# Expert weights of the second 128 tokens through a DRAM table instead of one-hot products

## The chip, the cores and the metric

The kernel runs on one core of a Trainium2 chip. The metric is device time in microseconds (us) of one execution. The engines are called by the profile's names: PE is TensorE's matmuls, PEld its weight loads, DVE is VectorE, ACT is ScalarE, POOL is GpSimd and SP is SyncE, which issues most DMA transfers. Each engine works through its instructions in the order in which the built program lists them.

## What is computed

One decoder layer for 256 tokens of width 1024, all in float32: a modulated norm, an input projection, retention and sparse attention, an output projection, then a second norm and an expert layer, and a last norm. The change lies in the expert layer, which is this, for 128 tokens at a time:

```python
q = (hblk @ w_q).reshape(B, TB, PEER_HEADS, 2, PEER_DHALF)
s = jnp.einsum('btphd,phnd->btphn', q, subkeys)
v, i = lax.top_k(s, PEER_TOPK)
cand = (v[..., 0, :, None] + v[..., 1, None, :])          # 16 x 16 sums per head
cidx = (i[..., 0, :, None] * PEER_NKEYS + i[..., 1, None, :])
tv, tj = lax.top_k(cand, PEER_TOPK)
eidx = jnp.take_along_axis(cidx, tj, axis=-1)
w = jax.nn.softmax(tv, axis=-1)
a = jax.nn.gelu(jnp.einsum('btd,btpkd->btpk', hblk, w_down[eidx]))
return jnp.einsum('btpk,btpkd->btd', w * a, w_up[eidx])
```

Each token has 8 heads with 16 experts each, out of 16384 experts. Within a head the 16 are all different; two heads of a token can choose the same expert, and then their weights add up.

## The kernel before

No expert's rows are gathered. The kernel goes through all 16384 experts in 128 tiles of 128, and multiplies with dense weights that are zero for experts that a token did not choose. The dense weights V lie in SBUF as 128 tiles (128 experts x 256 tokens): `VL` holds tiles 0 to 63, `VH` tiles 64 to 127.

The expert layer consists of units, in the order of the list `seq`: 16 query units (`wq`), 128 `down` units, 128 `up` units. Each unit reads 512 KB of weights (`load`, SP's queue, tile `raw`, three buffers), which ACT and DVE split into a rounded part `H` and a rest `L` (`split`, four buffers each), and then runs its products on PE three times (H, L and the other operand's rest). A `down` unit makes 24 matmuls of 256 columns, the gelu of a tile, and puts it into V or multiplies it in. An `up` unit takes V's tile, splits it into `a1` and `a2`, and makes 12 matmuls of 512 columns into four accumulators `acc_o`.

Beside the units two generators run, a piece at a time, by credits (a `wq` unit gives 1.7, a `down` unit 1.1 in the first phase and 1.15 in the second):

- `top_gen` (phase "top") finds the top 16 of each half of the product keys, sorts 50 candidate sums of each head (`top16`), and gets the chosen expert's number: a one-hot `oh` over 50 candidates for 16 places (128x800), its product `oe` with the candidates' numbers on POOL (L946), and the sum `ev` of that on DVE. A head's piece costs 2.1 credits. Then the softmax, and tables of the experts' high and low halves of seven bits and of the weights, transposed by PE. First tokens 0 to 127, then 128 to 255.
- `w_gen` (phase "w") turns the tables into V: for four tokens at a time one-hots `o1`, `o0` over 128 (DVE), their product with the weights in two parts `ow` (DVE and ACT), eight matmuls of 128 columns into bank `w`, and a copy or product into V. 64 groups for 256 tokens, 1.4 credits each.

When `w_gen` is through (phase "up"), the rest of `seq` becomes up and down units in turn, and then up units alone.

The order on each engine is the framework's: in the expert layer a scheduler lists the instructions by its own estimate, may move them forward past others, and puts in the waits; `issue_after` keeps the pieces of `top_gen` behind the last `L`. DVE, ACT and PE follow program order only where `order["on"]` names them, which in the expert layer is nowhere but in the tail. Most instructions of these engines carry line 80 (81 after the change), that of a helper, so the profile is read by tiles.

Of the kernel before, what the change touches and what calls it, by code (L numbers as in the profile page):

```python
# [24 lines left out]
F32 = mybir.dt.float32  # L25
# [11 lines left out]
P = 128  # L37
T = 256
# [18 lines left out]
SPL = 1  # L57
CT = 1.1
# [5 lines left out]
def build(tc, I, out, dbg=None, stop=None):  # L64
# [5 lines left out]
    class Ordered:  # L70
        """An engine whose instructions stay in program order while order["on"] has its name."""
# [52 lines left out]
    csd = mk(dpool, (1, D), F32, "csd")  # L124

# [105 lines left out]
    # 2 silu(c) on every partition  # L231
# [36 lines left out]
    # norm 1: the product that transposes a row block scales it too  # L268
# [38 lines left out]
    # projection blocks A (q | kc ks kw vc) and B (rq | vs vw gate)  # L307
# [92 lines left out]
    def rope(dst, src, tab, tt, nh, dh, v=0):  # L400
        """dst (SBUF) = rotated src (PSUM), nh heads of dh."""
# [24 lines left out]
    def half(c, post, nf=0):  # L426
        """A projection block of 512 columns; post(i) after each of its four units."""
# [81 lines left out]
    # NSA transposes  # L509
# [22 lines left out]
    # compressed keys and values  # L532
# [74 lines left out]
    # NSA attention  # L607
# [27 lines left out]
    def attn_unit(tt, p):  # L635
        """The scaled probabilities of heads p and 4 + p, transposed."""
# [74 lines left out]
    # retention: scores transposed, decayed  # L711
# [10 lines left out]

    nsa(0)
    nsa(1)

    # retention: values, group norm, swish gate
# [43 lines left out]
    # output projection, residual, norm 2: one half of the tokens after the other  # L770
# [79 lines left out]
    # ------------------------------------------------------------------- PEER  # L850
# [3 lines left out]
    vls = mk(vlo, (P, (NT // 2 + 4) * T), F32, "VL")  # L854
# [8 lines left out]
    tab = small[:, :T].bitcast(F16).rearrange("p (a b) -> p a b", a=2)  # L863
    tabw = small[:, T:T + T // 2].bitcast(F16)
    tabl = small[:, 2 * T:3 * T]
    iow = small[:, 3 * T:4 * T].bitcast(F16).rearrange("p (a b) -> p a b", b=WG)

    subT = mk(tk, (P, 16, P), F32, "subT")
    ioi = mk(tk, (P, P, WG), I32, "ioi")
    with tc.issue_after(spill.ins):  # L870
        nc.gpsimd.dma_start(subT, I["subT"])
        G.iota(ioi, pattern=[[1, P], [0, WG]], base=0, channel_multiplier=0)
    V.tensor_copy(iow, ioi)
    ioj = mk(tk, (P, NCAND, 16), BF, "ioj")
# [37 lines left out]
    def top_gen(sc):  # L912
        """Top 16 of each product key half, then of each head's candidates; then the tables."""
# [7 lines left out]
        for tt in range(2):  # L921
# [17 lines left out]
            pend = None  # L939
            for p in range(8):  # L940
                top16(cand[:, p, :], tv[:, p, :], tp[:, p, :], NCAND, "s3")
                V.tensor_copy(tpf[:, p, :], tp[:, p, :])
                oh = mk(tk, (P, NCAND, 16), BF, "oh", bufs=2)
                V.tensor_tensor(oh, ioj, tpf[:, p:p + 1, :].to_broadcast([P, NCAND, 16]), op=ALU.is_equal)
                oe = mk(tk, (P, NCAND, 16), F32, "oe", bufs=3)
                G.tensor_tensor(oe, oh, cidx[:, p, :, None].to_broadcast([P, NCAND, 16]), op=ALU.mult)  # L946
                if pend is not None:
                    V.tensor_reduce(ev[:, p - 1, :], pend.rearrange("p j k -> p k j"), axis=AX.X, op=ALU.add)
                pend = oe
                yield 2.1  # L950
            V.tensor_reduce(ev[:, 7, :], pend.rearrange("p j k -> p k j"), axis=AX.X, op=ALU.add)
            # softmax over the 16, its maximum first in the sorted values
            ex = mk(tk, (P, 8, 16), F32, "ex", bufs=2)
# [6 lines left out]
            ei = mk(tk, (P, P), I32, "ei", bufs=2)  # L960
            V.tensor_copy(ei, ev.rearrange("p a b -> p (a b)"))
            e1 = mk(tk, (P, 2, P), I32, "e1", bufs=2)
            V.tensor_scalar(e1[:, 0, :], ei, 7, None, op0=ALU.arith_shift_right)
            V.tensor_scalar(e1[:, 1, :], ei, 127, None, op0=ALU.bitwise_and)
            ef = mk(tk, (P, 2, P), F32, "ef", bufs=2)
# [8 lines left out]
            wt = mk(tk, (P, P), F32, "wt", bufs=2)  # L974
            S.activation(wt, b[:, 2, :], AF.Copy, scale=WSC)
            dump(f"e{tt}", ev)
            dump(f"w{tt}", ex)
            # the scaled weights in two parts of float16's precision
# [3 lines left out]

    def w_gen(ohp):
        """The dense weights of every expert and token, four tokens at a time, into VL and VH."""
        half = NT // 2
        for gi in range(T // 4):
# [47 lines left out]
    def gate_unit(m):  # L1034
        """A part of the second gate, in the place of weights that are used up; its row goes to DRAM."""
# [19 lines left out]
    def up_units(js, ap):  # L1055
        """Some experts' contributions, one half of the tokens after the other."""
        ops = []
        for j in js:
            h, l = splits.pop(("up", j))
            v = vtile(j)  # L1060
            a1 = mk(ap, (P, T), F32R, "a1", bufs=3)
# [6 lines left out]
        for tt in range(2):  # L1068
            tq = slice(tt * P, (tt + 1) * P)
            for hf in range(2):  # L1070
                # the very last sums in two halves, so that the first can go on
# [8 lines left out]
    # the order of the units on the tensor engine  # L1080
# [13 lines left out]
    def load_to(i):  # L1094
        while issued_u[0] <= i and issued_u[0] < len(seq):
            u = seq[issued_u[0]]
            load(u, I[u[0]][u[1]])
            issued_u[0] += 1
# [9 lines left out]

    gen = None
# [9 lines left out]
    while i < len(seq):  # L1119
# [20 lines left out]
        while gen is not None and credit > 0:  # L1140
            try:
# [11 lines left out]
                else:  # L1153
# [6 lines left out]
                    # the units already loaded stay first; then up and down in turn  # L1160
# [14 lines left out]
    # the tail: gated residual and the last norm  # L1175
# [87 lines left out]
def host_arrays(i):  # L1263
    """The inputs as the program reads them (layouts only) and constants of the shapes."""
# [56 lines left out]
```

## Time and profile before

| | us |
|---|---|
| median of 3 runs | 1040.93 |
| lowest and highest run | 1040.06, 1041.23 |
| span of the profiled execution, first to last instruction | 1037.9 |
| PE busy | 1009.2 (97%) |
| DVE busy | 760.4 (73%) |
| ACT busy | 606.8 (58%) |
| POOL busy | 61.5 (6%) |

The page gives the profiled execution's span and not its time from outside; the runs lie 2.2 to 3.3 us above that span. PE's busy time is that of pipelined matmuls with modelled ends, so a busy PE may still wait a little inside. The DMA engines moved 199 MB, 192 GB/s on average, most of it through SP's queue.

### The profile page before, as it was taken

What the parts mean: (1) busy time and instruction counts of PE and PEld (TensorE: products, weight loads), DVE (VectorE), ACT (ScalarE), POOL (GpSimd) and SP (SyncE); (2) the same over time, 40 slices, a digit from 0 to 9 for tenths busy, and PEclk for the clock granted to TensorE, in tenths of its full rate; (3) what the DMA queues carried; (4) which work ended last, traced back from release to release, by engine and by line L of the source; (5) the groups of instructions that cost most, each with busy time, mean ns of one, the idle gap of its engine ahead of it and who ended that gap; (6) DMA issues with size and microseconds to landing.
All of it is one profiled execution on the core that took longest, in us unless ns stands there. A gap on an engine that the chain in (4) does not pass through costs nothing.

```text
span 1037.9 us, 17713 instructions
## 1 busy us (share of the span) xinstructions
PE 1009.2 (97%) x6580; PEld 902.1 (87%) x6582; DVE 760.4 (73%) x1653; ACT 606.8 (58%) x1244; POOL 61.5 (6%) x53
## 2 busy tenths in 40 slices
PE   7999999999998889999999999999999999999995
PEld 6876687999998889999999999988888888888884
DVE  7988888899778786667777777665955556565665
ACT  7544884555436357777777777645445555545453
POOL 1040000000331310000000000000000000000001
PEclk9999999999999999999999999999999999999998
DMA  9998753546555444444444444567976666666661
GB/s 367 352 350 335 244 181 136 168 152 183 168 149 174 144 152 135 151 147 143 148 142 144 143 143 143 156 230 231 317 234 193 197 190 214 190 199 188 198 189 57
DMA packets 56184, 199.19 MB, mean 192 GB/s; under 512 B 7305, under 2 KB 7585, under 8 KB 55713
## 3 DMA queue, kind: packets, MB, share of 16 engines
q1 hardware_dynamic: 55200, 193.59, 58.3%
q0 software_dynamic: 752, 4.20, 1.1%
q8 instruction: 51, 0.84, 0.3%
q14 instruction: 37, 0.30, 0.1%
q10 hardware_dynamic: 144, 0.26, 0.1%
HBM read 195.92 MB, written 2.11 MB: 191 GB/s over the span
## 4 chain that ended last, share of the span: by engine, by line
PE 84%; DVE 9%; POOL 3%; ACT 1%; issue 1%; DMA 0%; SPq 0%; DVEq 0%; POOLq 0%; ACTq 0%
PE acc L80 54%; PE dn L80 9%; PE w L80 7%; PE C L80 5%; PE O L80 4%; POOL oe L946 3%; PE S L80 3%; PE T L80 2%; DVE ev L80 2%; DVE L L80 2%; DVE oh L80 1%; DVE tp L80 1%; DVE VL L80 1%; DVE adaraw L80 0%; DMA xn<-in_x_dram 0%
## 5 line engine op out<-in xcount | busy, mean ns | idle before, releaser
L80 DVE TENSOR_TENSOR L<-raw,H 128x1024 fp32r<-128x1024 f32 x284 | 346.4, 1221 | 119.5 <-ACT H L80 114.9
L80 ACT ACTIVATE H<-raw 128x1024 fp32r<-128x1024 f32 x284 | 300.0, 1058 | 172.4 <-PE acc L80 132.6
L80 PE MATMUL acc<-H,a 128*128 128x512 f32 (+1 forms) x1030 | 315.9, 388 | 0.0
L80 PE MATMUL acc<-hH,H 128*128 128x256 f32 x800 | 230.8, 289 | 0.0
L80 PE MATMUL acc<-hH,L 128*128 128x256 f32 x800 | 226.6, 283 | 3.3 <-DVE L L80 3.3
L80 PEld LDWEIGHTS acc<-H,a 128*128 128x128 f32 x1030 | 193.0, 188 | 39.9
L80 PE MATMUL acc<-hL,H 128*128 128x256 f32 x800 | 226.6, 283 | 0.0
L80 PE MATMUL acc<-L,a 128*128 128x512 f32 (+1 forms) x515 | 199.7, 388 | 0.0
L80 PEld LDWEIGHTS acc<-hH,L 128*128 128x128 f32 x800 | 152.9, 191 | 4.1 <-DVE L L80 4.1
L80 PEld LDWEIGHTS acc<-hH,H 128*128 128x128 f32 x800 | 153.5, 192 | 0.1
L80 PEld LDWEIGHTS acc<-hL,H 128*128 128x128 f32 x800 | 153.2, 192 | 0.2 <-DVE hL L80 0.2
L80 PEld LDWEIGHTS acc<-L,a 128*128 128x128 f32 x515 | 96.7, 188 | 19.7
L80 ACT ACTIVATE ow<-o,VL 128x128 f16<-128x128 f16 x256 | 104.5, 578 | 5.2 <-DVE o L80 5.2
L80 PE MATMUL dn<-hH,L 128*128 128x256 f32 x352 | 99.8, 283 | 4.4 <-DVE L L80 4.4
L80 PE MATMUL dn<-hH,H 128*128 128x256 f32 x352 | 101.5, 288 | 0.4 <-ACT H L80 0.4
L80 PE MATMUL dn<-hL,H 128*128 128x256 f32 x352 | 99.6, 283 | 0.0
L80 PEld LDWEIGHTS dn<-hH,L 128*128 128x128 f32 x352 | 67.3, 191 | 5.0 <-DVE L L80 5.0
L80 PE MATMUL w<-ow,o 128*128 128x128 f16 x512 | 71.0, 296 | 0.0
L80 PEld LDWEIGHTS dn<-hH,H 128*128 128x128 f32 x352 | 67.6, 192 | 0.6 <-ACT H L80 0.6
L80 PEld LDWEIGHTS dn<-hL,H 128*128 128x128 f32 x352 | 67.4, 192 | 0.0
L80 PEld LDWEIGHTS <-o 128*128 128x128 f16 x512 | 51.9, 118 | 3.4
L80 DVE TENSOR_TENSOR ow<-o,VL 128x512 f16<-128x512 f16 x64 | 26.9, 420 | 36.9 <-PE w L80 36.9
(333 smaller groups left out, 1213.5 us busy)
## 6 DMA issues: line engine op xcount, KB each, us to landing
raw<-in_down_dram SPq DMA_DIRECT2D x128, 512.0 KB, 3.6
raw<-in_up_dram SPq DMA_DIRECT2D x128, 512.0 KB, 3.7
adaraw<-in_wadaT_dram SPq DMA_DIRECT2D x40, 512.0 KB, 8.0
raw<-in_wq_dram SPq DMA_DIRECT2D x16, 512.0 KB, 3.7
raw<-in_win_C_dram SPq DMA_DIRECT2D x12, 512.0 KB, 5.2
rawA<-in_win_A_dram SPq DMA_DIRECT2D x8, 512.0 KB, 9.6
raw<-in_wout_dram SPq DMA_DIRECT2D x8, 512.0 KB, 4.7
VL<-in_wadaT_dram SPq DMA_DIRECT2D x8, 512.0 KB, 4.6
```

The source lines that it names most:

```text
L80: i = fn(*a, **kw)
L946: G.tensor_tensor(oe, oh, cidx[:, p, :, None].to_broadcast([P, NCAND, 16]), op=ALU.mult)
```

## The change

Only tokens 0 to 127 keep the one-hots of `w_gen` (32 groups instead of 64). For tokens 128 to 255:

- A table `wd2` of 16384 x 128 float32 (8.4 MB) lies in DRAM, one row for each expert and one column for each of these tokens. It is filled with zeros by eight transfers of 1 MB from a tile `zero`, issued on POOL's queue.
- `top_gen` takes these tokens first. It sorts all heads (0.8 credits each), does the softmax into `exd`, and then finds a head's expert numbers (1.8 credits each), with `oe` on DVE instead of POOL. For tokens 128 to 255 the number times 128 plus the token gives the address `eid`, and `put_weights` adds the head's weights to the table: 16 indirect transfers on POOL's queue, each with 128 addresses of 4 bytes (one for each token). The 16 of a head may run together; the next head's wait until they have landed.
- With each load of an `up` tile goes a read of 128 rows of the table (64 KB, tile `wt2`, two buffers) on SP's queue, which waits for the last head's additions. `up_units` multiplies V's columns 128 to 255 by it.
- `down` units put the gelu of tokens 128 to 255 straight into V.

```diff
+    wd2 = mk(dpool, (NT * P, P), F32, "wd")
+    wd = wd2.rearrange("a (b o) -> (a b) o", o=1)
...
+    zero = mk(pe_, (P, ZC), F32, "zero")
+    G.memset(zero, 0.0)
+    wz = wd2.rearrange("(p a) b -> p (a b)", p=P)
+    for i in range(NT * P // ZC):
+        G.dma_start(wz[:, i * ZC:(i + 1) * ZC], zero)
...
-        for tt in range(2):
+        for tt in (1, 0):
...
-                oe = mk(tk, (P, NCAND, 16), F32, "oe", bufs=3)
-                G.tensor_tensor(oe, oh, cidx[:, p, :, None].to_broadcast([P, NCAND, 16]), op=ALU.mult)
-                if pend is not None:
-                    V.tensor_reduce(ev[:, p - 1, :], pend.rearrange("p j k -> p k j"), axis=AX.X, op=ALU.add)
-                pend = oe
-                yield 2.1
+                yield 0.8
...
+            for p in range(8):
+                oh = mk(tk, (P, NCAND, 16), BF, "oh", bufs=2)
+                V.tensor_tensor(oh, ioj, tpf[:, p:p + 1, :].to_broadcast([P, NCAND, 16]), op=ALU.is_equal)
+                oe = mk(tk, (P, NCAND, 16), F32, "oe", bufs=2)
+                V.tensor_tensor(oe, oh, cidx[:, p, :, None].to_broadcast([P, NCAND, 16]), op=ALU.mult)
+                V.tensor_reduce(ev[:, p, :], oe.rearrange("p j k -> p k j"), axis=AX.X, op=ALU.add)
+                if tt:
+                    V.tensor_scalar(ev[:, p, :], ev[:, p, :], float(P), tokf, op0=ALU.mult, op1=ALU.add)
+                    V.tensor_copy(eid[:, p, :], ev[:, p, :])
+                    put_weights(p)
+                yield 1.8
+            if tt:
+                continue
...
+    def put_weights(p):
+
+        group = []
+        for k in range(16):
+            i = G.indirect_dma_start(wd, bass.IndirectOffsetOnAxis(ap=eid[:, p, k:k + 1], axis=0),
+                                     exd[:, p, k:k + 1], None, compute_op=ALU.add)
+            for o in group:
+                tc.declare_no_dep(i.ins, o.ins, reason="a head's places all differ")
+            for o in placed:
+                tc.add_manual_dep(i.ins, o.ins.name, sync, reason="the head before has been added")
+            group.append(i)
+        placed[:] = group
...
-        for gi in range(T // 4):
+        for gi in range(P // 4):
...
+            V.tensor_tensor(v[:, P:], v[:, P:], wts.pop(j), op=ALU.mult)
...
+            if u[0] == "up":
+                w = mk(apool, (P, P), F32, "wt2", bufs=2)
+                i_ = Q.dma_start(w, wd2[u[1] * P:(u[1] + 1) * P, :])
+                for o in placed:
+                    tc.add_manual_dep(i_.ins, o.ins.name, sync, reason="all heads have been added")
+                wts[u[1]] = w
```

In the built program three places show what moved. The first is POOL's queue at the program's start, before the first rope (tile `kn`); `cs_p` and `keys` are tiles that the attention clears, `csd` is a copy of a row to DRAM. Before:

```order
L534 MEMSET kcT_772 128x32
L626 MEMSET cs_p_949 128x256
L196 MEMSET epsd_85 128x1
L277 DMA csd_73<-cs_98 16x1x64
L413 TENSOR_TENSOR kn_579<-sq_596 128x384
```

After:

```order
L537 MEMSET kcT_773 128x32
L727 MEMSET zero_934 128x2048
L629 MEMSET cs_p_960 128x256
L730 DMA wd_74<-zero_934 128x2048 x8
L280 DMA csd_73<-cs_99 16x1x64
L199 MEMSET epsd_86 128x1
L416 TENSOR_TENSOR kn_580<-sq_597 128x384
```

The zeros stand in the code behind the retention scores, but go out at the very start, before anything that POOL waits for.

The second place is SP's queue at the loads of `down` tiles 45 to 49 (units 61 to 65), with the semaphores that each row waits for; DMAHW are SP's own transfers, DMASW those of POOL's queue. Before:

```order
L80 DMA raw_4336<-in_down_dram 128x1024 [waits DMAHW3_49,DVE_49]
L80 DMA raw_4368<-in_down_dram 128x1024 [waits DMAHW4_49,DVE_49]
L80 DMA raw_4412<-in_down_dram 128x1024 [waits DMAHW5_49,DVE_49]
L80 DMA raw_4444<-in_down_dram 128x1024 [waits DMAHW6_49,DVE_49]
L80 DMA raw_4491<-in_down_dram 128x1024 [waits DMAHW7_49,DVE_49]
```

After:

```order
L81 DMA raw_4475<-in_down_dram 128x1024 [waits DMAHW4_49,DVE_49]
L81 DMA raw_4512<-in_down_dram 128x1024 [waits DMAHW5_49,DVE_49]
L81 DMA raw_4549<-in_down_dram 128x1024 [waits DMAHW6_49,DVE_49]
L81 DMA wt_1250_6984<-wd_74 128x128 [waits DMASW4_49,DMASW3_49,DMASW5_49,DMASW2_49,DMASW6_49,DMASW1_49,DMASW7_49,DMASW0_49,PE_49]
L81 DMA wt_1261_7056<-wd_74 128x128
L81 DMA raw_4581<-in_down_dram 128x1024 [waits DMAHW7_49,DVE_49]
L81 DMA raw_4618<-in_down_dram 128x1024 [waits DMAHW0_49,DVE_49]
```

The reads of the table were moved forward from the up units to here, some 40 units earlier: the two `wt2` buffers take the place of `exd` and `eid`. The values waited for are those after the last of the 128 additions.

The third place is DVE's queue at the same units, in the last heads of the top phase. Before:

```order
L80 TENSOR_TENSOR L_4415<-raw_4292,H_4414 128x1024 [waits DMAHW7_49,PE_49,Activation_49]
L80 CAST tpf_3899<-tp_3898 128x16 [waits DVE_49]
L80 TENSOR_TENSOR oh_4407<-ioj_1964,tpf_3899 128x800 [waits DVE_49]
L80 TENSOR_TENSOR L_4447<-raw_4336,H_4446 128x1024 [waits DMAHW0_49,PE_49,Activation_49]
L80 TENSOR_REDUCE ev_3900<-oe_4409 128x16 [waits Pool_49]
```

After:

```order
L81 TENSOR_TENSOR L_4584<-raw_4475,H_4583 128x1024 [waits DMAHW0_49,PE_49,Activation_49]
L81 TENSOR_TENSOR oh_4613<-ioj_1981,tpf_4075 128x800
L81 TENSOR_TENSOR oe_4615<-oh_4613,cidx_3994 128x800 [waits DMASW4_49,DMASW3_49,DMASW5_49,DMASW2_49,DMASW6_49,DMASW1_49,DMASW7_49,DMASW0_49,DVE_49]
L81 TENSOR_TENSOR L_4621<-raw_4512,H_4620 128x1024 [waits DMAHW1_49,PE_49,Activation_49]
L81 TENSOR_REDUCE ev_4076<-oe_4615 128x16 [waits DVE_49]
L81 TENSOR_TENSOR VL_1963<-VL_1963,wt_1250_6984 128x128 [waits DMAHW3_49]
L81 TENSOR_TENSOR VL_1963<-VL_1963,wt_1261_7056 128x128 [waits DMAHW4_49]
L81 TENSOR_TENSOR L_4653<-raw_4549,H_4652 128x1024 [waits DMAHW2_49,PE_49,Activation_49]
```

DVE no longer waits for POOL's `oe`, but for all transfers of POOL's queue, ahead of the L of unit 62; the products with the table's tiles follow there.

## Rows read from the trace of the kernel before

**Rows 1.** The page's first part: busy us, share of the span, instructions.

```profile
PE 1009.2 (97%) x6580; PEld 902.1 (87%) x6582; DVE 760.4 (73%) x1653; ACT 606.8 (58%) x1244; POOL 61.5 (6%) x53
```

**Rows 2.** Stages: length, busy us (instructions) of each engine, PEclk, DMA share, GB/s.

```profile
183.00:262.00 79.00, 79.00 (x664) 78.81 (x663) 74.10 (x310) 40.91 (x68) 1.30 (x1) 1.00 0.55 167
262.00:315.00 53.00, 50.41 (x416) 49.80 (x415) 41.72 (x101) 24.42 (x37) 17.22 (x8) 1.00 0.50 150
315.00:325.00 10.00, 9.33 (x78) 9.33 (x79) 10.00 (x37) 5.35 (x12) 0.00 (x0) 1.00 0.74 244
325.00:382.00 57.00, 50.62 (x410) 49.17 (x410) 45.38 (x108) 25.01 (x40) 19.25 (x8) 1.00 0.48 143
382.00:662.00 280.00, 280.00 (x2345) 276.56 (x2344) 201.81 (x449) 212.48 (x556) 0.00 (x0) 1.00 0.48 145
...
678.00:1024.00 346.00, 346.00 (x1530) 286.51 (x1530) 213.63 (x273) 173.51 (x256) 3.10 (x6) 1.00 0.66 207
```

**Rows 3.** Chain that ended last, top phase: start us, us, engine and tile.

```profile
291.87 1.56 DVE ev L80
...
296.31 2.42 POOL oe L946
298.75 1.54 DVE ev L80
```

**Rows 4.** The same chain in the one-hot stage.

```profile
384.88 0.95 PE w L80 x8
385.83 2.87 PE dn L80 x24
```

**Rows 5.** The same chain in the prefix, two rounds of k.

```profile
28.69 1.38 PE O L80 x6
...
33.56 1.38 PE O L80 x6
```

**Rows 6.** Stretches of the prefix, columns as in rows 2.

```profile
17.50:20.90 3.40, 3.21 (x16) 2.30 (x15) 3.23 (x5) 3.37 (x6) 0.00 (x0) 1.00 1.03 412
...
24.30:55.00 30.70, 30.70 (x151) 25.93 (x151) 28.57 (x51) 16.17 (x26) 0.00 (x0) 1.00 0.93 345
55.00:100.00 45.00, 44.80 (x238) 28.64 (x238) 38.47 (x93) 19.35 (x51) 10.99 (x9) 1.00 0.93 358
100.00:183.00 83.00, 80.66 (x516) 62.22 (x516) 69.93 (x164) 59.99 (x148) 2.12 (x3) 1.00 0.58 191
```

**Rows 7.** DVE by form, 255 to 385 us: busy, mean ns | idle before, releaser.

```profile
L80 DVE TENSOR_TENSOR L<-raw,H 128x1024 fp32r<-128x1024 f32 x40 | 48.5, 1218 | 2.8 <-ACT H L80 1.4 <-issue 1.3
L80 DVE TENSOR_REDUCE ev<-oe 128x16 f32<-128x800 f32 x16 | 24.8, 1550 | 20.4 <-POOL oe L946 20.4
...
L80 DVE CAST tpf<-tp 128x16 bf16<-128x16 uint32 x16 | 2.7, 167 | 0.1
...
L80 DVE TENSOR_TENSOR VL<-wt,VL 128x128 f32<-128x128 f32 x1 | 0.3, 283 | 0.0
```

**Rows 8.** POOL's instructions in order of time: start, us [idle before, releaser].

```profile
0.88 0.53 POOL L395 MEMSET sq<- 128x512 f32 x1
...
8.47 0.68 POOL L277 DMA_DIRECT2D csd<-cs  x1 [3.82 <-DVE t L80]
...
179.62 0.54 POOL L871 DMA_DIRECT2D subT<-in_subT_dram  x1
...
303.18 2.40 POOL L946 TENSOR_TENSOR oe<-oh,cidx 128x800 f32<-128x800 bf16 x1 [4.46 <-DVE oh L80]
310.11 1.56 POOL L946 TENSOR_TENSOR oe<-oh,cidx 128x800 f32<-128x800 bf16 x1 [4.52 <-DVE oh L80]
```

**Rows 9.** DMA issues: count, KB each, median us from issue to landing.

```profile
out_dram<-VL SPq DMA_DIRECT2D x3, 256.0 KB, 2.0
...
csd<-cs POOLq DMA_DIRECT2D x1, 4.0 KB, 5.0
```

**Rows 10.** DVE in order of time, beside POOL's oe of 310.11 us.

```profile
311.70 1.53 DVE L80 TENSOR_REDUCE ev<-oe 128x16 f32<-128x800 f32 x1 [1.73 <-POOL oe L946]
```

More of the change, by code (lines that the diff above doesn't have):

```diff
@@ L57 @@
 SPL = 1
+ZC = 2048
 CT = 1.1
@@ L853, in build @@
     vlo = es.enter_context(tc.tile_pool(name="vlo", bufs=1, reuse_waits="tile"))
-    vls = mk(vlo, (P, (NT // 2 + 4) * T), F32, "VL")
+    vls = mk(vlo, (P, NT // 2 * T + 576), F32, "VL")
     VL = vls[:, :NT // 2 * T].rearrange("p (a b) -> p a b", a=NT // 2)
@@ L862, in build @@
     WG = 4
[L863 to L866, printed above, removed]
+    tab = small[:, :P].bitcast(F16).rearrange("p (a b) -> p a b", a=2)
+    tabw = small[:, P:P + P // 2].bitcast(F16)
+    tabl = small[:, 192:320]
+    iow = small[:, 320:576].bitcast(F16).rearrange("p (a b) -> p a b", b=WG)
     subT = mk(tk, (P, 16, P), F32, "subT")
     ioi = mk(tk, (P, P, WG), I32, "ioi")
+    tok = mk(tk, (P, 1), I32, "tok")
+    tokf = mk(tk, (P, 1), F32, "tokf")
     with tc.issue_after(spill.ins):
@@ L872, in build @@
         G.iota(ioi, pattern=[[1, P], [0, WG]], base=0, channel_multiplier=0)
+        G.iota(tok, pattern=[[P, 1]], base=0, channel_multiplier=1)
     V.tensor_copy(iow, ioi)
+    V.tensor_copy(tokf, tok)
+    exd = mk(tabs, (P, 8, 16), F32, "exd")
+    eid = mk(tabs, (P, 8, 16), I32, "eid")
     ioj = mk(tk, (P, NCAND, 16), BF, "ioj")
@@ L938, in top_gen @@
             ev = mk(tk, (P, 8, 16), F32, "ev", bufs=2)
-            pend = None
             for p in range(8):
@@ L942, in top_gen @@
                 V.tensor_copy(tpf[:, p, :], tp[:, p, :])
-                oh = mk(tk, (P, NCAND, 16), BF, "oh", bufs=2)
-                V.tensor_tensor(oh, ioj, tpf[:, p:p + 1, :].to_broadcast([P, NCAND, 16]), op=ALU.is_equal)
-                oe = mk(tk, (P, NCAND, 16), F32, "oe", bufs=3)
-                G.tensor_tensor(oe, oh, cidx[:, p, :, None].to_broadcast([P, NCAND, 16]), op=ALU.mult)
-                if pend is not None:
-                    V.tensor_reduce(ev[:, p - 1, :], pend.rearrange("p j k -> p k j"), axis=AX.X, op=ALU.add)
-                pend = oe
-                yield 2.1
-            V.tensor_reduce(ev[:, 7, :], pend.rearrange("p j k -> p k j"), axis=AX.X, op=ALU.add)
-            ex = mk(tk, (P, 8, 16), F32, "ex", bufs=2)
+                yield 0.8
+            ex = exd if tt else mk(tk, (P, 8, 16), F32, "ex", bufs=1)
             V.tensor_tensor(ex, tv, tv[:, :, 0:1].to_broadcast([P, 8, 16]), op=ALU.subtract)
@@ L959, in top_gen @@
             V.tensor_tensor(ex, ex, sm[:, :, None].to_broadcast([P, 8, 16]), op=ALU.mult)
-            ei = mk(tk, (P, P), I32, "ei", bufs=2)
+            for p in range(8):
[11 more added lines that the diff above has]
+                continue
+            ei = mk(tk, (P, P), I32, "ei", bufs=1)
             V.tensor_copy(ei, ev.rearrange("p a b -> p (a b)"))
-            e1 = mk(tk, (P, 2, P), I32, "e1", bufs=2)
+            e1 = mk(tk, (P, 2, P), I32, "e1", bufs=1)
             V.tensor_scalar(e1[:, 0, :], ei, 7, None, op0=ALU.arith_shift_right)
             V.tensor_scalar(e1[:, 1, :], ei, 127, None, op0=ALU.bitwise_and)
-            ef = mk(tk, (P, 2, P), F32, "ef", bufs=2)
+            ef = mk(tk, (P, 2, P), F32, "ef", bufs=1)
             V.tensor_copy(ef, e1)
@@ L973, in top_gen @@
             S.activation(tab[:, :, tq], b[:, 0:2, :], AF.Copy)
-            wt = mk(tk, (P, P), F32, "wt", bufs=2)
+            wt = mk(tk, (P, P), F32, "wt", bufs=1)
             S.activation(wt, b[:, 2, :], AF.Copy, scale=WSC)
-            dump(f"e{tt}", ev)
-            dump(f"w{tt}", ex)
             V.tensor_copy(tabw[:, tq], wt)
@@ L981, in top_gen @@
             yield 1.0
+    sync = mybir.DependencyInfo(mybir.DependencyClass.Sync, mybir.DependencyReason.DATA)
+    placed = []
+    def put_weights(p):
[9 more added lines that the diff above has]
+        placed[:] = group
     def w_gen(ohp):
         half = NT // 2
-        for gi in range(T // 4):
+        for gi in range(P // 4):
             t0 = gi * 4
@@ L1107, in split_to @@
             splitted[0] += 1
+    wts = {}
     gen = None
```

## Prediction

> **What bounds the kernel now.** The busy shares come first [rows 1]: TensorE (PE) is busy for 97% of the span. That is an average, so the stages come next, all at full granted clock [rows 2]. Before 183 us stands the prefix. From 183 to 262 us PE has no idle time. From 262 to 382 us (the rest of the selection of experts, called top phase below) it idles for 2.6 + 0.7 + 6.4 = 9.6 us. From 382 to 662 us (one-hots) and from 678 to 1024 us (up products) it has none. The chain of waits tells who sets the pace in the top phase [rows 3]: not PE but VectorE (DVE), in a ring of L, oh, POOL's oe and ev that comes round every 298.75 - 291.87 = 6.88 us, once a head. After 382 us the chain is PE alone [rows 4]: a down unit takes 2.87 us, a group of four tokens' one-hot products 0.95 us. In the prefix PE follows a period of 33.56 - 28.69 = 4.87 us for one k [rows 5], and the DMA engines are just as full: share 1.03 from 17.5 to 20.9 us and 0.93 from 24.3 to 100 us [rows 6]. So PE's work pays one for one after 382 us, DVE's work counts from 262 to 382 us, and DMA bytes count before 100 us.
>
> **One-hots for 128 tokens only.** 32 of the 64 groups of `w_gen` go. Each has 0.95 us of PE on the chain [rows 4], and PE has no idle time there [rows 2]: 32 x 0.955 = 30.6 us are gained. DVE's and ACT's share of these groups was hidden and gives nothing.
>
> **The top phase.** `oe` moves from POOL to DVE. In the ring DVE idles for 20.4 / 16 = 1.3 us a head, waiting for POOL, and works 5.6 us, two L among it [rows 7]. The product over 800 elements lies between the row of 128 (283 ns) and L's of 1024 (1218 ns) [rows 7]; on the line between them it is 0.98 us. Half of the heads get two short operations more, each near the 167 ns of the cast [rows 7]. By the code's credits a head now spans 2.6 / 1.1 = 2.36 units instead of 1.91, so 0.36 L (0.4 us) are added: 5.6 + 0.98 + 0.4 = 7.0 us, or 7.3 with the short operations, for 2.36 units, that is 3.0 to 3.1 us for a unit. PE wants 2.87. DVE falls behind by 0.17 us in each of 16 x 2.36 = 38 units, 6.4 us, while the four L buffers let it run 4 x 2.87 = 11.5 us ahead. So PE's idle 9.6 us should go (bounds: none of it or all of it; I take all, since 6.4 is under 11.5).
>
> **Read-back and the extra product.** 128 products of 128x128 on DVE at 0.283 us [rows 7] make 36 us, 128 reads of 64 KB make 8.4 MB, and a down unit's gelu stays in two pieces on ACT. From 382 us on DVE works 201.8 of 280 us and 213.6 of 346 us, ACT less than 77%, the DMA engines 0.48 to 0.66 [rows 2]. I cost all three at nothing. If that cover is gone, it is in the one-hot stage: DVE at 72% plus about two products in 3.83 us (15%) would be near 87%; I allow 0 to 8 us.
>
> **The zeros.** The order shows POOL's memset and the eight writes of 1 MB ahead of everything that POOL waits for. A memset of 512 columns takes 0.53 us [rows 8], so the one of 2048 takes about 2 us and the writes start near 6.5 us. 8.39 MB at 350 to 410 GB/s [rows 6] is 20 to 24 us of all DMA engines, in a stretch where 0.07 of 31 us, some 2 us, are to spare up to 55 us, and where PE and DMA are equally full. DVE's second rope, an ACT copy and SP's load of `wv` wait for the end of the writes, so they can't spread over the later, emptier stretch; and from 55 to 183 us PE idles for only 2.5 us [rows 6], so a late start is not won back. I take 20 us, with 10 (writes that fit the gaps better) and 28 (rows of 8 KB that hold off loads of 4 KB rows, and so the first k) as ends.
>
> **The 128 indirect additions and who waits for them.** POOL issues 16 for a head and then waits until these have landed. It starts when the first `eid` is ready, with L of unit 32 (16 query units and then down units, counted from 0). Two queues wait for the last of the 128. SP waits at the first read of the table, behind unit 63's load: all further weight loads stand behind it. DVE waits after unit 61's L. That is 29 units after the start, far ahead of the up units for which the table is read, because the scheduler moved the reads and products up to the place where memory becomes free. 29 units at 3.04 us are 88 us, and PE lives for some 6 us more from L tiles in store: 94 us are covered. When the wait ends, DVE has an oe (0.98) and an L (1.22) ahead of PE: 3 us with ACT's part.
>
> What POOL needs is not in the trace; I bound it from both sides. Issue: at least the 0.54 us of a plain transfer of 128 rows; the row that is cut into small pieces (csd) took 0.68 us [rows 8]. At most 2.4 us, POOL's longest instruction over 128 partitions [rows 8]. Landing: 2.0 us, as for the output, to 5.0 us, as for csd's 4 KB [rows 9]. POOL is slower beside DVE: oe took 1.56 us when DVE stood still for it and 2.40 us when an L ran beside it [rows 8, 10], a factor of 1.54. DVE is nearly always busy here. I take 0.68 x 1.54 = 1.04 us, since 128 addresses of 4 bytes are nearest to csd's pieces, and 3.5 us, the middle, to land: 128 x 1.04 + 8 x 3.5 = 161 us. PE stands still for 161 - 94 = 67 us.
>
> The Trainium skill (SBUF — State Buffer, "SBUF: two separate sides") says that DVE and GpSimd share a port pair under an exclusive lock, and that descriptors written by GpSimd starve under it. The trace agrees as far as the two times of oe go; no row shows it for a transfer. Without that factor the sum would be 128 x 0.68 + 28 = 115 us and the stall 21 us.
>
> **Sum.** 1037.9 - 30.6 - 9.6 + 20 + 67 + 3 = 1087.7 us of span. The median of the runs is 3.0 us above the profiled span (1040.93), so about **1091 us**. A measurement of this kernel tells some 0.2% (2 us) from no change.
>
> **Rivals.**
> 1. *The additions are cheap, and the kernel is faster.* Issue 0.54 and landing 2.0 us give 128 x 0.54 + 16 = 85 us, less than the 94 covered. No stall, nothing to refill: 1037.9 - 40.2 + 20 + 3.0 = **1021 us**. It decides below 111 us for all 128 (0.65 us each with 3.5 us to land), where the stall and its 3 us eat the 20 us that remain. For it: POOL's direct transfers in [rows 8]. Against it: none of them has 128 separate destinations, and DVE was not saturated beside them. Chance 0.20. The Trainium skill (DMA: Bandwidth & Descriptors, "Anatomy of one DMA — SWDGE (gpsimd) path") speaks for this case: about 2.0 us fixed for a transfer, and many descriptors before their making counts. No run here shows it for indirect ones yet.
> 2. *The additions are heavy*, since each reads DRAM before it writes, or POOL reads addresses slowly: 2.4 us each and 5.0 us to land are 128 x 2.4 + 40 = 347 us, a stall of 253 us and **1277 us**. For it: POOL's slow rows beside DVE. Against it: eight transfers may be under way at once. Chance 0.18 for anything above 1200 us or near it.
> 3. *The zeros are hidden* and the stall is as forecast: 1091 - 20 = **1071 us**. For it: DMA shares under 1.0 from 24 us on. Against it: PE's period and the DMA engines' are equal there. Chance 0.12.
> 4. The forecast, with a stall of 20 to 150 us: 0.50.
>
> **How the numbers follow.** The cheap case reaches up to the border of no change, so faster by over 0.2% has 0.19, within 0.2% 0.03 (the narrow band near 111 us), slower 0.78. The range from 1019 to 1200 us takes in the cheap case at its price and POOL times up to some 270 us (1.9 us each with 3.5 us to land); what is left out is most of rival 2 and a little below 1019. The bounds of the zeros (10 to 28) and of the read-back (0 to 8) lie inside.
>
> **What would show it.** In the profile after: a hole of PE, DVE, ACT and SP together near 380 to 450 us, its end released by POOL's queue, and POOL's indirect transfers one behind the other from about 300 us; their mean time decides between 1, 2 and the forecast. The first query unit near 203 us instead of 183 and a k period above 4.87 us for the zeros. No POOL in the ring of the top phase, and PE without gaps up to the hole. 256 matmuls of `w` instead of 512 and down units every 3.83 us behind the hole. Wrong would be: a PE without the hole, a hole that begins elsewhere (a wait that I did not find), or up units slower than before, which I cost at nothing.

## The result, and the profile after

The changed kernel takes **1208.6 us** (median of 4 runs, 1206.2 to 1212.6) against 1040.5 us before: a ratio of 1.162 (95% interval 1.160 to 1.165), slower. The forecast was 1091 us with 1019 to 1200 as range: the sign and the place of the loss were right, the size was not.

The page of the changed kernel, its span, busy shares and some of the lines of 40 slices (30.1 us each), stands against [rows 1]:

```profile
span 1205.6 us, 17346 instructions
...
PE 986.8 (82%) x6323; PEld 879.0 (73%) x6323; DVE 746.2 (62%) x1647; ACT 555.1 (46%) x1077; POOL 241.3 (20%) x175
...
PE   5799999999999000000999999999999999999996
...
DVE  4788887999997000001887786655855555555556
...
POOL 3030000000877777777000000000000000000001
PEclk7899999999999555555999999999999999999998
```

PE is busy 22 us less than before and the span is 168 us longer. The slices show why: six of them are empty on PE, and DVE does nothing in five of these and a tenth in the sixth, while POOL works on. Five stretches (length, busy us and instructions of PE, PEld, DVE, ACT and POOL, then granted clock, DMA share, GB/s) answer to [rows 2, 6]:

```profile
25.00:50.00 25.00, 18.50 (x66) 14.59 (x67) 12.98 (x21) 8.73 (x14) 0.00 (x0) 0.75 1.02 420
225.00:375.00 150.00, 150.00 (x1256) 150.00 (x1255) 146.30 (x478) 78.28 (x119) 58.78 (x32) 1.00 0.66 173
388.00:571.00 183.00, 1.44 (x13) 1.24 (x11) 1.42 (x2) 0.00 (x0) 141.28 (x91) 0.51 0.21 1
571.00:600.00 29.00, 25.38 (x192) 25.06 (x193) 26.99 (x52) 15.22 (x32) 0.00 (x0) 0.90 0.76 236
600.00:625.00 25.00, 25.00 (x211) 24.72 (x211) 19.33 (x48) 21.22 (x56) 0.00 (x0) 1.00 0.57 164
```

The first is the zeros: DMA full at 420 GB/s, PE short of weights and at a granted clock of 0.75. The second is the top phase, in which PE no longer idles. The third is the hole. The fourth is its tail: 192 matmuls in 29 us, where the fifth, the same work at full pace, makes 211 in 25. Who holds the engines in the hole is told by the waits between 380 and 580 us (engine, tile, what it waited for: us, times, longest):

```profile
ACT H L81 <- DMA raw<-in_down_dram: 191.8, 3, 190.4
DVE oe L81 <- DMA wd<-exd,eid: 186.3, 1, 186.3
PEld acc L81 <- DVE L L81: 182.5, 1, 182.5
PE acc L81 <- DVE L L81: 182.3, 1, 182.3
```

PE waits for an L of DVE; DVE waits for the indirect transfers, but **in front of an oe**, an instruction of the selection that touches no table. ACT waits for weights, because SP stands at its first read of the table. POOL in order of time, around the start of the fourth head (start, us, [idle before, releaser]), answers to [rows 8]:

```profile
377.83 3.68 POOL L1007 DMA_INDIRECT wd<-exd,eid  x1 [0.30 <-issue]
381.82 2.43 POOL L1007 DMA_INDIRECT wd<-exd,eid  x1 [0.31 <-issue]
384.55 1.55 POOL L1007 DMA_INDIRECT wd<-exd,eid  x1 [0.30 <-issue]
...
406.83 1.55 POOL L1007 DMA_INDIRECT wd<-exd,eid  x1 [0.30 <-issue]
410.85 1.55 POOL L1007 DMA_INDIRECT wd<-exd,eid  x1 [2.46 <-issue]
```

From the moment DVE stands still (383.3 us) every later transfer takes 1.55 to 1.57 us and 0.30 us pass before the next. Between heads 2.4 to 2.6 us pass, in which POOL waits for the landing. Beside a busy DVE a transfer took up to 3.68 us. The first starts at 300.06 us. The chain that ended last (start, us, what) has the last one together with its landing, and behind the hole a read of the table:

```profile
566.28 3.03 DMA wd<-exd,eid
...
587.18 4.57 DMA wt<-wd
```

So the last has landed at 569.3 us: POOL needs 269 us for the 128.

### The profile page after: what moved, and what is told of

The parts are those of the page before. It is cut to its first block, busy times and chain, and to the rows that moved or that the text cites. A ratio compares the mean times of both kernels' runs of the same rounds, so it can differ in the third digit from the quotient of the medians.

```text
span 1205.6 us, 17346 instructions
## 1 busy us (share of the span) xinstructions
PE 986.8 (82%) x6323; PEld 879.0 (73%) x6323; DVE 746.2 (62%) x1647; ACT 555.1 (46%) x1077; POOL 241.3 (20%) x175
## 3 DMA queue, kind: packets, MB, share of 16 engines
q0 software_dynamic: 20336, 12.66, 7.1%
## 4 chain that ended last, share of the span: by engine, by line
PE 45%; DMA 4%; DVE 3%; issue 1%; POOL 1%; ACT 0%; DVEq 0%; SPq 0%; ACTq 0%
PE acc L81 33%; PE dn L81 10%; DMA wt<-wd 3%; PE w L81 3%; DVE L L81 1%; POOL wd L1007 1%; DVE VL L81 1%; DMA raw<-in_down_dram 0%; DVE VH L81 0%; DVE ev L81 0%; DMA wd<-exd,eid 0%; ACT VL L81 0%; DVE oe L81 0%; DVE r30v L81 0%; ACT H L81 0%
## 5 line engine op out<-in xcount | busy, mean ns | idle before, releaser
L81 PE MATMUL acc<-hH,L 128*128 128x256 f32 x616 | 175.8, 285 | 182.3 <-DVE L L81 182.3
L1007 POOL DMA_INDIRECT wd<-exd,eid x128 | 211.3, 1651 | 156.6 <-DVE exd L81 100.1
L81 PE MATMUL acc<-hH,H 128*128 128x256 f32 x616 | 178.6, 291 | 0.0
L81 PE MATMUL acc<-hL,H 128*128 128x256 f32 x616 | 175.8, 286 | 0.0
L81 PE MATMUL dn<-hH,H 128*128 128x256 f32 x536 | 152.9, 285 | 1.4 <-ACT g L81 1.4
L81 PE MATMUL dn<-hL,H 128*128 128x256 f32 x536 | 151.7, 283 | 0.0
L81 PE MATMUL dn<-hH,L 128*128 128x256 f32 x536 | 151.7, 283 | 0.0
L81 PEld LDWEIGHTS dn<-hH,H 128*128 128x128 f32 x536 | 102.9, 192 | 3.7 <-ACT g L81 2.5
L81 PEld LDWEIGHTS dn<-hL,H 128*128 128x128 f32 x536 | 102.7, 192 | 1.2
L81 DVE SCALAR_TENSOR_TENSOR adaraw<-adaraw,cs 128x1024 f32<-128x1024 f32 x40 | 48.3, 1216 | 12.4 <-DMA adaraw<-in_wadaT_dram 12.4
```

Of the source, the lines that this page charges most:

```text
L81: i = fn(*a, **kw)
L1007: i = G.indirect_dma_start(wd, bass.IndirectOffsetOnAxis(ap=eid[:, p, k:k + 1], axis=0), exd[:, p, k:k + 1], None, compute_op=ALU.add)
```

## The experiments

First the two waits. In the built program exd has bytes 88064 to 88576 and eid 89088 to 89600 of each partition, and the sixth oe of the *first* 128 tokens was packed into 88448 to 91648. That place is free only when the last addition has read its operands. The text on the order above gave the place of exd and eid to the two `wt2` buffers instead; in the built program the first of these lie at bytes 166272 and up, on tiles of H. So there are two causes to take apart: the place of the oe, and the reads of the table that were moved some 40 units forward on SP.

**a1_reads_late**: each read on SP behind its own unit's weight load.

```
-                i_ = Q.dma_start(w, wd2[u[1] * P:(u[1] + 1) * P, :])
+                with tc.issue_after(last["load"].ins):
+                    i_ = Q.dma_start(w, wd2[u[1] * P:(u[1] + 1) * P, :])
```

> The changed kernel with one edit: each read of the table stands on SP's queue behind its own up unit's weight load, so no read and no product is moved forward. Theory P (the prediction's words: both queues wait because the scheduler moved the reads and products forward): both waits go with the reads to the first up unit, near 550 us; the additions end near 570 us there, so the hole of 182 us shrinks to 20 to 50 us and the time is 1050 to 1080 us. Theory S (the wait on DVE has nothing to do with the reads: in the built program the sixth oe of the first 128 tokens has SBUF bytes 88448 to 91648 of each partition, and exd and eid, which the additions read, have 88064 to 88576 and 89088 to 89600, so the packer gave this oe a place that is free only after the last addition): the hole stays, from about 388 to 570 us, and the time is 1200 to 1215 us.

Measured: 1223.0 us (ratio 1.176, 1.173 to 1.178). The hole stays:

```profile
DVE oe L81 <- DMA wd<-exd,eid: 184.4, 1, 184.4
```

Theory S holds, the prediction's account of DVE's wait falls: the reads are not what DVE waits for. The 14 us on top of the changed kernel's time are lost later, in the up stage, where PE idles for 5.7 us between 1000 and 1200 us and makes 807 matmuls there (the changed kernel 884 from 980 to 1180 us); a4, d1 and e1 below show why.

**a2_own_place**: exd and eid as columns of VL's tile, made 256 columns wider for them, that nothing takes later; the reads stay moved forward.

```
-    exd = mk(tabs, (P, 8, 16), F32, "exd")
-    eid = mk(tabs, (P, 8, 16), I32, "eid")
+    exd = small[:, 576:704].rearrange("p (a b) -> p a b", a=8)
+    eid = small[:, 704:832].bitcast(I32).rearrange("p (a b) -> p a b", a=8)
```

> The changed kernel with one edit: exd and eid get bytes of their own at the end of VL's tile (1 KB a partition), which nothing takes later; the reads of the table stay where they were moved, 40 units ahead. Theory: DVE no longer waits, but SP still waits at the first read with all later weight loads behind it, and three raw and four H and L tiles in store let PE go on for at most 7 units more (20 us): hole from 388 to 410 us until 570 us, 1190 to 1215 us. Rival (SP's wait is covered by what is loaded, DVE's place alone made the hole): hole under 50 us, below 1080 us.

Measured: 1209.9 us (ratio 1.163, 1.161 to 1.166). The same hole with another holder:

```profile
DVE VL L81 <- DMA wt<-wd: 193.3, 15, 182.8
ACT H L81 <- DMA raw<-in_down_dram: 234.1, 27, 188.0
```

Now it is SP's read with the weights behind it, and on DVE a product with the table that was moved forward; no oe waits any more. The rival is out.

**a3_both**: both edits.

> Both edits at once: own place for exd and eid, and each read behind its own up load. Theory: each of two waits alone makes the hole, so only both together take it away; then the first queue that waits is SP at the first up unit, near 550 us. POOL's additions end near 570 us if they keep the 1.86 us of the hole (8 x 32 us from 300 us), or 580 to 600 us if they take longer beside a busy DVE: a hole of 20 to 50 us, 1040 to 1075 us. Rival (accumulating transfers slow every queue of DMA while they run, so the weights come late): hole small, but PE below full from 390 to 570 us, above 1080 us.

Measured: 1085.3 us (ratio 1.043, 1.040 to 1.047), 10 us above the expected band. One hole is left, in front of the first up unit, where PE works 9.39 of 50 us:

```profile
550.00:600.00 50.00, 9.39 (x67) 9.19 (x66) 5.21 (x10) 4.97 (x12) 29.89 (x20) 0.59 0.28 34
```

So either wait alone keeps the whole hole, and only both together remove it: 123 us went. Before that hole PE is at full (24.9 to 25.0 of each 25 us from 400 to 550 us) while POOL adds, so the additions don't hold up the weights.

**a4_both_ups_last**: a3, and all down units before the up units.

```
-                        new += [("up", j), uu]
-                        j += 1
+                        new.append(uu)
```

> Both edits, and all down units stand before all up units, so the first read of the table comes near 690 us. Theory: no hole at all; the changed kernel's 1208 us less 184 us of hole and some 5 us behind it (refill, half clock) is 1015 to 1025 us, faster than before by 1.5 to 2.4%. Rival 1 (the additions take over 3 us each beside a busy DVE, 128 of them over 390 us): a hole is left before the first up unit, above 1040 us. Rival 2 (ups that no longer alternate with downs lose time, since each read and load follows close behind the other): PE below full from 690 us, 1030 to 1060 us.

Measured: 1046.1 us (ratio 1.004, 1.003 to 1.006). The hole is gone, but the time is 21 us above the expected band. The loss is in the up stage. PE made fewer matmuls there than in the same stage before (1530 in 346 us, 442 in 100 [rows 2]; here 402), and SP stood in front of a read until an earlier read into the same place had landed (us, times, longest). In the built program 118 of the 128 reads go to one and the same place, in a1 and a3 all 128, in the changed kernel no more than 66:

```profile
750.00:1000.00 250.00, 239.63 (x1005) 184.64 (x1004) 146.29 (x249) 116.14 (x167) 0.54 (x1) 1.00 0.66 199
...
SPq L81 <- DMA wt<-wd: 135.5, 109, 3.7
```

**d1_pool_reads**: a4 with the reads on POOL's queue, into six places, and each product kept behind the L that is written before it in the code.

```
-                w = mk(apool, (P, P), F32, "wt2", bufs=2)
-                with tc.issue_after(last["load"].ins):
-                    i_ = Q.dma_start(w, wd2[u[1] * P:(u[1] + 1) * P, :])
+                c = 64 + u[1] % 6 * P
+                w = small[:, c:c + P]
+                i_ = G.dma_start(w, wd2[u[1] * P:(u[1] + 1) * P, :])
...
-            V.tensor_tensor(v[:, P:], v[:, P:], wts.pop(j), op=ALU.mult)
+            with tc.issue_after(last["L"].ins):
+                V.tensor_tensor(v[:, P:], v[:, P:], wts.pop(j), op=ALU.mult)
```

> As a4_both_ups_last, but the 128 reads of the table are issued by POOL instead of SP, into six places in VL's tile. In a4 PE made 101 matmuls in 25 us of the up stage where the changed kernel makes 112, and SP stood still 109 times (135 us) at a read of the table whose place was still in use, with the next weight load behind it. Theory: the reads on SP are what cost there; on POOL, which has nothing else to do after the additions, they hold up no weight load, PE has 112 matmuls in 25 us again, 128 units of 2.68 us instead of some 2.85: 20 to 25 us less than a4, 1020 to 1027 us. Rival (the up stage is slower because ups stand alone there, 512 KB of weights and 64 KB of table for each 2.68 us): no gain, 1040 to 1050 us.

Measured: 1018.6 us (ratio 0.979, 0.978 to 0.981), 27.6 us under a4 and faster than before.

```profile
750.00:1000.00 250.00, 249.98 (x1098) 205.43 (x1098) 161.18 (x277) 125.20 (x185) 47.37 (x87) 1.00 0.68 212
```

1098 matmuls instead of 1005 in the same 250 us: the table's reads as a4 has them were the loss, not that ups stand alone. But d1 changes the queue and the places at once.

**e1_sp_six_places**: a4 with d1's six places, the reads still on SP.

```
-                w = mk(apool, (P, P), F32, "wt2", bufs=2)
+                c = 64 + u[1] % 6 * P
+                w = small[:, c:c + P]
```

> As a4_both_ups_last (1046 us), with the reads still on SP's queue behind their own weight load, but into the six places of d1_pool_reads (1019 us), so it takes apart what d1 changed at once. Theory Q (the queue: a read on SP holds up the next weight load whatever its place): 1036 us and more, SP still stands 100 us and more at its reads. Theory W (the place: SP stood because a read's place was still in use, in a4 all shared few places; the queue itself costs little, 0.32 us of SP for a read): below 1026 us, PE back at some 440 matmuls in 100 us of the up stage.

Measured: 1026.8 us (ratio 0.988, 0.986 to 0.989); theory W missed its border by 0.8 us. SP's waits for the reads of the table are gone from its list, and PE is nearly at pace:

```profile
750.00:1000.00 250.00, 248.46 (x1089) 203.28 (x1088) 157.94 (x269) 123.23 (x181) 0.54 (x1) 1.00 0.72 215
```

So of the 27.6 us between a4 and d1, 19.3 are the places (with one place a read waits until the read before it has landed and its product has used it, and the next weight load stands behind), and the other 8.3 us come with SP's queue and with d1's fixed order of the products, which were not taken apart.

**d2_pool_reads_late_zeros**: d1, with the zeros behind the second clearing of cs_p (POOL, near 83 us).

```
-    zero = mk(pe_, (P, ZC), F32, "zero")
-    G.memset(zero, 0.0)
...
     nsa(1)
+    with tc.issue_after(last["csp"].ins):
+        zero = mk(pers, (P, 512), F32, "zero")
+        G.memset(zero, 0.0)
+        wz = wd2.rearrange("(p a) b -> p (a b)", p=P)
+        for i in range(NT * P // ZC):
+            G.dma_start(wz[:, i * ZC:(i + 1) * ZC].rearrange("p (a b) -> p a b", b=512),
+                        zero[:, None, :].to_broadcast([P, ZC // 512, 512]))
```

> As d1_pool_reads, and the zeros are written later: POOL's memset (512 columns, repeated as source) and the eight writes of 1 MB stand behind the second clearing of cs_p, near 83 us, where the DMA engines have room (0.58 busy from 100 to 183 us in the kernel before). Theory: the zeros cost the changed kernel its 19 us because they stand in a stretch where PE and DMA are both full; moved, 15 to 19 us come back: first query unit near 185 us, 1002 to 1010 us, faster than before by 3 to 4%. Rival (8.4 MB of writes cost their time wherever they stand, since the weights of the output projection are loaded there): 0 to 5 us gained, 1016 to 1027 us.

Measured: **999.4 us** (ratio 0.961, 0.959 to 0.962), 19.2 us under d1. The prefix is whole again, at full clock:

```profile
25.00:50.00 25.00, 25.00 (x125) 21.26 (x124) 24.49 (x46) 14.23 (x21) 0.00 (x0) 1.00 1.03 409
```

This is the change with its three added costs taken off, 41 us faster than before, beside 30.6 + 9.6 = 40.2 us that the prediction gave for the one-hots and the top phase. The order of down and up units differs from before as well; what that alone does to the kernel before was not tried.

Then the price of one transfer, with one run for each of three variants. **b1_plain_write** is a4 without the addition, **b2_half_addresses** and **c3_16_addresses** are a4 with 64 and 16 partitions instead of 128:

```
-                                     exd[:, p, k:k + 1], None, compute_op=ALU.add)
+                                     exd[:, p, k:k + 1], None)
```

```
-            i = G.indirect_dma_start(wd, bass.IndirectOffsetOnAxis(ap=eid[:, p, k:k + 1], axis=0),
-                                     exd[:, p, k:k + 1], None, compute_op=ALU.add)
+            i = G.indirect_dma_start(wd, bass.IndirectOffsetOnAxis(ap=eid[:P // 2, p, k:k + 1], axis=0),
+                                     exd[:P // 2, p, k:k + 1], None, compute_op=ALU.add)
```

c3 has 16 in place of P // 2.

> As a4_both_ups_last, but the 128 indirect transfers write instead of adding, so a place that occurs in two heads keeps only one weight. Theory (POOL's own work on 128 addresses sets the 1.6 to 1.9 us, what the memory does with the data is not seen): each still 1.6 to 1.9 us on POOL with 0.3 us between, first to last 300 to 325 us, and the whole within 0.5% of a4. Rival (the addition, a read and a write of DRAM, is what costs): below 1.1 us each, first to last below 200 us; the landing between heads falls as well.

> As a4_both_ups_last, but each indirect transfer takes 64 partitions, so the weights of tokens 192 to 255 are left out. Theory of a price for each address: a plain transfer of 128 rows takes 0.54 us on POOL, an indirect one 1.55 us where DVE stands still; if the 1 us of difference goes by addresses, 64 of them take 1.05 us, and beside a busy DVE 1.1 to 1.35 us against a4's 1.90. Rival (a fixed price for an indirect transfer): 1.5 us and more, first to last 300 us as in a4.

> As a4_both_ups_last, but each adding transfer takes 16 partitions (the weights of tokens 144 to 255 are left out). With 64 addresses the shortest took 1.41 us, with 128 1.55, 2.2 ns an address. Theory (a fixed price of 1.27 us and 2.2 ns an address): shortest 1.28 to 1.33 us. Rival (the price goes in steps by groups of addresses, or the last 16 engines' packets set it): below 1.1 us.

Measured, in the order a4, b1, b2, c3 (shortest, median and longest in ns; first and last start):

```profile
L1007 POOL DMA_INDIRECT wd<-VL x128: 1551/1672/2767, 298.9 to 601.3; - x128
```

```profile
L1007 POOL DMA_INDIRECT wd<-VL x128: 962/972/2624, 300.2 to 509.0; - x128
```

```profile
L1007 POOL DMA_INDIRECT wd<-VL x128: 1412/1463/2625, 300.2 to 570.8; - x128
```

```profile
L1007 POOL DMA_INDIRECT wd<-VL x128: 1282/1378/2762, 298.6 to 560.8; - x128
```

b1: both expectations were wrong in part: the rival had the price right (below 1.1 us), but first to last took 209 us and not under 200. A plain write takes 0.96 us, an adding one 1.55, so 0.59 us of each is the addition, and POOL is held for it. The packets of POOL's queue (packets, MB, share of the DMA engines) tell the two apart as well; a4, b1 and b2:

```profile
q0 software_dynamic: 20336, 12.66, 7.3%
```

```profile
q0 software_dynamic: 6000, 12.66, 3.4%
```

```profile
q0 software_dynamic: 12144, 12.63, 5.7%
```

Half the addresses (128 x 64) make 8192 packets fewer, one for each address; so a4's additions make 16384 of its 20336, 3952 belong to other transfers, and b1's 128 writes make 2048, 16 each. b2: the expected 1.05 us is refuted; halving the addresses takes 0.14 us off, 2.2 ns each. From these two the price is 1.27 us fixed and 2.2 ns an address; that gives 1.31 us for 16, and c3 showed 1.28. The times of a4, b1, b2 and c3 (1046.1, 1046.4, 1042.8, 1043.5 us) are near each other, since none has a hole that POOL's time could lengthen.

What a busy DVE adds is seen in the same traces. In a4, an L on DVE and the transfer that starts 0.08 us into it:

```profile
566.69 1.22 DVE L81 TENSOR_TENSOR L<-raw,H 128x1024 fp32r<-128x1024 f32 x1 [1.45 <-ACT H L81]
566.77 2.58 POOL L1007 DMA_INDIRECT wd<-VL  x1 [0.30 <-issue]
```

1.14 us of the L are left, and the transfer takes 1.03 us longer than 1.55. In the changed kernel 17 transfers start inside an L, and 16 of them are longer by what is left of that L less 0.11 to 0.13 us. The longest of all (3.68 us) starts in an oh that an L and an oe follow without a gap, and lasts 2.13 us longer where the oe ends 2.25 us after its start. Beside an idle DVE the price was 1.55 to 1.57 us (95 transfers of the changed kernel, 16 of a4), and no higher for the 20 of a4 that start inside a SCALAR_TENSOR_TENSOR and the 8 of both that start inside an ev. So it is not a factor: a transfer that starts inside an L, oh or oe waits until DVE is through with it. POOL's two oe in [rows 8] fit the same form: the slow one starts at 303.18 us, inside this L of the kernel before, with 0.99 us of it left, and takes 2.40 - 1.56 = 0.84 us longer.

```profile
302.95 1.22 DVE L80 TENSOR_TENSOR L<-raw,H 128x1024 fp32r<-128x1024 f32 x1
```

Last, whether the hole is POOL's time less a cover. **c1_after_plain_write** and **c2_after_half_places** are the changed kernel itself with its waits, c1 with b1's edit, c2 with 8 of 16 places of a head:

```
-        for k in range(16):
+        for k in range(8):
```

> The changed kernel with its two waits left as they are, and the 128 transfers write instead of adding (a place that occurs in two heads keeps one weight). b1 showed 0.96 us for a plain transfer beside a still DVE against 1.55 for an adding one. Theory (the hole is POOL's time less the cover, one for one): three heads by about 380 us, five more of 16 x (0.96 + 0.30) + 2.4 = 22.6 us, last landing near 497 us instead of 569.6; the hole from 388 us ends 70 to 76 us earlier, 1132 to 1140 us. Rival (something else than POOL's time, such as the memory's own read and write of 4 bytes, sets the end): 1190 us and more.

> The changed kernel with its waits, and only 8 of a head's 16 places are added (half of the second 128 tokens' weights are left out). Theory (POOL's time less the cover): 64 transfers; heads of 8 x 1.86 + 2.4 = 17.3 us beside a still DVE and some 20 us beside a busy one, last landing near 450 us; a hole of 55 to 65 us in place of 182, 1080 to 1095 us. That is near the additions' time of the prediction (161 us), so it also shows what stall its rule, X - 94, gives for such a time: some 56 us for X of 150. Rival (the cover is much smaller or larger than 86 to 94 us): a hole under 35 or over 85 us.

Measured: c1 1131.4 us (ratio 1.089, 1.087 to 1.092), 0.6 us below the expected band. The transfers of the changed kernel and of c1 (shortest, median, longest in ns; first and last start):

```profile
L1007 POOL DMA_INDIRECT wd<-exd,eid x128: 1551/1552/3677, 300.1 to 566.3; - x128
```

```profile
L1007 POOL DMA_INDIRECT wd<-exd,eid x128: 965/971/2635, 298.7 to 488.2; - x128
```

The last starts 78 us earlier, and the time is 77 us shorter: one for one. c2 took 1113.8 us (ratio 1.071, 1.069 to 1.073), where 1080 to 1095 were expected. POOL's part was right (transfers from 300.0 to 440.5 us), the cover was not:

```profile
DVE VL L81 <- DMA wt<-wd: 99.5, 11, 90.1
...
PE acc L81 <- DVE L L81: 87.4, 2, 86.5
```

In this build it is a moved product with the table at which DVE stands, and it stands earlier: PE stopped at 363.5 us, 63 us after the first transfer in place of 89. So the hole is POOL's time less a cover, but the cover is a property of where the first waiter happens to be put, and X - 94 is no rule.

## Why the prediction failed, step by step

- **One-hots and top phase: right.** PE is full from 225 to 375 us; an oe on DVE took 988 ns, 0.98 were estimated. d2 shows the sum of the two gains, 41 us, whole.
- **Zeros: right.** 20 us were taken, d1 less d2 is 19.2. That a late start is not won back was right too. In d2 the writes start at 92 us, and PE is busy for all of 80 to 130 us.
- **Read-back at nothing: nearly right here, by luck of its place.** In the changed kernel the reads run ahead, and PE lost 1.35 us between 700 and 800 us, and some of the tail below; in a4, on SP in step with the loads, they cost 27.6 us more than on POOL (d1), most of it (19.3) for want of places. The cover named (DVE, ACT and DMA shares) was not the one that counts: that is how far ahead SP may issue a read.
- **The price of a transfer: the step that failed.** The working put a transfer near csd's 0.68 us and multiplied by 1.54 for a busy DVE: 128 x 1.04 + 8 x 3.5 = 161 us. Measured were 128 x 1.65 = 211 us on POOL, 120 x 0.30 = 36 us between the transfers of a head (no term in the sum), 20 us between heads and 1.5 us until the last had landed: 269 us. Of the 108 us that were missing, 78 are the transfer itself and 36 the step from one to the next, while the landings were 6.6 us cheaper. Even beside a still DVE the price was 1.55 us, so the base was wrong before any factor: neither row that was chosen as an end for a cheap transfer has an address list or an addition.
- **The factor for a busy DVE: right in direction, wrong in form.** The working gave a busy DVE 128 x 0.36 = 46 us. Measured over 1.55 us a transfer, the 128 took 13 us more: 1.95 us each on average in the first head, 1.55 in the last five beside a DVE that stood still. It is a wait for the end of the DVE instruction in hand, as the transfers above show, and the two oe from which the factor was taken fit that form. Such a wait can still come in full each time: in a4's last head POOL falls into step with L, and a transfer takes 2.56 us on average. The Trainium skill (SBUF — State Buffer, "SBUF: two separate sides") has GpSimd's descriptor writes wait while DVE holds the port pair they share. The trace agrees in the form, a wait to the end of a DVE instruction; that this port pair is the cause was not isolated.
- **What was fixed in the price.** It is 1.27 us for which POOL itself is held by each adding transfer; why it takes that long stays open. The Trainium skill (DMA: Bandwidth & Descriptors, "Anatomy of one DMA — SWDGE (gpsimd) path") gives a transfer some 2.0 us of fixed cost, most of it until the write is confirmed, and lets many descriptors be made before their cost shows. The trace agrees in both: 2.4 to 2.6 us pass between the later heads, and an address costs 2.2 ns.
- **Cover and refill.** PE stopped at 389.4 us, 89.4 us after the first transfer (94 were taken), and 2.4 us passed from the landing to PE's restart at 571.8 us (3 taken). The tail behind it was missing from the sum: 192 matmuls until 600 us where 238 would fit at the pace of the next stretch, 5.4 us. The granted clock (1.00 until PE stopped, 0.50, the lower of its two levels, from 396 us on) stayed there until 576 us, 4 us into the new work; another 2.9 us are idle between 592 and 600 us. The chain leads from there back over DVE to the read of the table that was 4.57 us under way.
- **Sum.** The hole with its restart is 182.3 us where 70 were forecast: 112.3 more. Less 0.8 for the zeros, plus 5.4 of tail, plus 1.35 between 700 and 800 us: 118.3, and the spans differ by 1205.6 - 1087.7 = 117.9 us.
- **Why the range missed.** Its upper end was 1200 us for additions of about 270 us. They took 269, and the time still came out 9 us above, mostly by 5 us of cover and 5 us of tail. Rival 2 (heavy additions, 0.18; it took in times near 1200 us) was the right direction at too high a price. Of its two reasons the addition is worth 0.59 us of 1.55, and the slow reading of addresses at most 128 x 2.2 ns = 0.28 us; that the first is DRAM being read was not shown. 0.50 for the forecast was too sure of a price that no row showed.
- **DVE's wait: right place, wrong cause.** The order showed the wait and its queue; the reason given (reads and products moved forward) is refuted by a1, and with own bytes (a2) no oe waits any more. An unrelated oe had been packed onto the bytes that the transfers read. The moved reads and products are a second wait of the same length (a2), and in c2 the earlier one.

## What to carry to other kernels

A long chain of indirect transfers is priced by its count: here 128 adding ones, in eight groups that wait for each other, took 266 to 305 us from the first start to the last end, and 128 plain writes 190 to 210 us. An eighth of the addresses (c3) still took 265 us where a4 took 305. So ask first what is queued behind the last one. A buffer that such a transfer reads stays taken until it lands; give it bytes of its own, since any tile that gets its place inherits the wait, on an engine that has nothing to do with it. And reads that share a queue with weight loads need places enough to run ahead: the same 128 reads cost 28 us more between the loads on SP with hardly more than one place than from POOL with six, and 8 us more on SP with six.

## What was not expected of the hardware

- An indirect transfer of 128 single elements keeps POOL 0.96 us when it writes and 1.55 us when it adds, where a direct one (subT in [rows 8]) takes 0.54 us. Adding makes one packet an address, writing 16 a transfer.
- The addresses hardly count: 16, 64 and 128 of them took 1.28, 1.41 and 1.55 us.
- Starved of weights by the zeros, PE stood without work from 18 to 21 us, and its granted clock read 0.50 from 21 to 28 us and again from 38 to 42 us (0.75 over 25 to 50 us); with the zeros moved it stayed at 1.00. So here PE lost to the missing weights and ran at the lower clock after it had stood; how much of the 19.2 us each took was not taken apart.
